# Row fetches tied to the dense expert steps, and gate one-hots built four tokens at a time, in a PEER layer

## The chip, the core and the metric

One core of a Trainium2 chip runs the whole program. The metric is the device time of one execution in microseconds (us).

## The reference, cut to what matters

The model is a two-layer hybrid block followed by a second block; its last layer is a PEER layer (product-key retrieval of experts), and only that layer is touched here. For each of 512 tokens and 8 heads it scores 128 + 128 half keys, takes the best 16 of each half, adds them to 16 x 16 candidates, takes the best 16 of those and forms a softmax gate over them. So each token uses 8 x 16 = 128 of 16384 experts:

```python
cand = (s_top[:, :, 0, :, None] + s_top[:, :, 1, None, :]).reshape(n_tok, PEER_HEADS, -1)
cand_idx = (i_top[:, :, 0, :, None] * PEER_NKEYS + i_top[:, :, 1, None, :]).reshape(...)
best, pos = lax.top_k(cand, PEER_TOPK)
idx = jnp.take_along_axis(cand_idx, pos, axis=-1)
gate = jax.nn.softmax(best, axis=-1)
act = gelu(einsum("td,thkd->thk", tb, u_tab[ib]))      # u_tab, v_tab: 16384 x 1024, float32
out = einsum("thk,thkd->td", gb * act, v_tab[ib])
```

## The kernel before

**Two ways through the same layer.** The first 128 tokens take the sparse way (`gathered`, L1434): for each of their 128 slots an indirect DMA on POOL's queue (L1444) brings one row of 1024 floats for each of the 128 tokens (512 KB), first from table `pur`, later from `pvr`. A `pur` row is multiplied with the token's hidden vector and summed on DVE (L1450); four such dots go through a Gelu on ACT (L1454) and the gate (L1455); then each `pvr` row is added to `acc`, scaled, on DVE (L1459). All rows use four buffers of one tag, `er`. That makes 256 fetches and 256 uses.

The other 384 tokens take the dense way: all 16384 experts are computed with matmuls and masked by a gate matrix. The 128 chunks of 128 experts are in 16 groups of 8. For each group there are 8 *e-steps* (`expert`, L1482: a 512 KB weight tile is loaded by SP at L78, split into a high and a low part on ACT, L84, and DVE, L85, 24 matmuls of 384 columns follow at L106, then a product on DVE, L1486, and a Gelu on ACT, L1488; POOL multiplies with the gate tile, L1515; ACT, L92, and DVE, L93, split the result into `eh` and `el`) and 8 *m-steps* (weight tile as before, 24 matmuls that read `eh` and `el`, and an addition to the residual on DVE, L1535). So a weight tile goes with 24 matmuls in both kinds. The groups run in the order 4 to 15, then 0 to 3. The 32 chunks of groups 0 to 3 are computed early, inside the stage that builds the gate matrix (`ahead`, L1493), and stored; their e-steps later only load the stored activations, so these four groups have matmuls in their m-steps alone. The gate tile `gt` of a group is loaded by SP at L1508, with two buffers, so the load for a group is issued when POOL has done the last product of the group two places earlier.

**The gate stage** (`pairs`, L1574) runs over four tiles of 128 tokens. For each tile: candidates on POOL, the top 16 of each head on DVE, the two half positions from `pos` by a shift and a mask on unsigned integers with a cast each (L1590 to L1593), two one-hot selections over 128 x 2048 (`eq`: compare on DVE, L1595, product on POOL, L1596, sum on DVE, L1597), and the softmax. For tile 0 this ends in `eidx` and `egate`, the indices for the fetches. For tiles 1 to 3 the gate matrix is built token by token: `lt` is the one-hot row of the first half index times the gate (DVE, L1633, one instruction per token), `rt` the one-hot of the second half index (two tokens on ACT by Square and Relu, L1625 and L1629; two on POOL, L1627), their outer product is a matmul of 128 columns (L1634), and four tokens are copied out of PSUM by ACT (L1635). There are 96 such packs of four tokens, 32 per tile; a pack sits in a block of four, and each of the 24 blocks is stored to DRAM.

**What sets the order.** The program is written as one sequence, and the framework's planner orders each engine's instructions by its own estimate of time: of the instructions that it takes to be ready, the one that stands first in the program goes first. `gathered` is a generator; `more(n)` takes n of its steps, a step being one fetch and its use. The calls put 10 steps over the 8 e-steps of a group and 8 over its m-steps, but nothing ties them there: a fetch goes out as soon as a buffer is free, and a use as soon as its row is expected.

Of the kernel before, what the change touches and what calls it, by code (L numbers as in the profile page):

```python
# [9 lines left out]
F = mybir.dt.float32  # L10
# [16 lines left out]
D = 1024  # L27
# [3 lines left out]
SPT = 128  # L31
DW = 512 - SPT
EARLY = 4
EPS = 1e-6
# [9 lines left out]
class K:  # L44
# [1389 lines left out]
    def gathered(self, ht):  # L1434

        nc, mp, a = self.nc, self.mp, self.a
        NB = 4
        acc = mp.tile([128, D], F, name="acc")
        nc.gpsimd.memset(acc, 0.0)
        self.acc = acc  # L1440

        def fetch(table, s):
            r = mp.tile([128, D], F, name="er", tag="er", bufs=4)
            nc.gpsimd.indirect_dma_start(r, None, a[table], bass.IndirectOffsetOnAxis(ap=self.eidx[:, s:s + 1], axis=0))  # L1444
            return r
        for b in range(0, 128, NB):
            dot = mp.tile([128, NB], F, name="dot", bufs=2)
            for i in range(NB):
                r = fetch("pur", b + i)
                nc.vector.tensor_tensor_reduce(out=r, in0=r, in1=ht, scale=1.0, scalar=0.0, op0=OP.mult, op1=OP.add,  # L1450
                                               accum_out=dot[:, i:i + 1])
                if i == NB - 1:
                    w = mp.tile([128, NB], F, name="ew", bufs=2)
                    nc.scalar.activation(w, dot, AF.Gelu)  # L1454
                    nc.vector.tensor_mul(w, w, self.egate[:, b:b + NB])  # L1455
                yield
            for i in range(NB):
                r = fetch("pvr", b + i)
                nc.vector.scalar_tensor_tensor(acc, r, w[:, i:i + 1], acc, op0=OP.mult, op1=OP.add)  # L1459
                yield  # L1460

    def peer(self):
# [6 lines left out]
        with tc.tile_pool(name="peer", bufs=1) as mp:  # L1469
            self.mp = mp  # L1470
            io = mp.tile([128, 144], F, name="io")
            nc.sync.dma_start(io, a["iota"])
            sel = [mp.tile([128, DW], F, name=f"sel{i}") for i in range(4)]
            ht = self.by_token(rc)
# [22 lines left out]
            with tc.tile_pool(name="topk", bufs=1) as tp:  # L1497
                self.topk(tp, hh, hl, rr, io, sel, gd, ahead)
            with tc.tile_pool(name="exp", bufs=1) as ep:
                groups = list(range(EARLY, 16)) + list(range(EARLY))  # L1500
                for g in groups:
                    wh, wl = [], []
                    last = g == groups[-1]
                    for e in range(8):
                        j = g * 8 + e
                        if e == 0:
                            gt = ep.tile([128, DW // TB, 8, TB], F, name="gt", bufs=2)
                            nc.sync.dma_start(gt, gd[:, :, j:j + 8, :])  # L1508
                        if g < EARLY:
                            act = mp.tile([128, DW], F, name="act", bufs=4)  # L1510
                            nc.sync.dma_start(act, ad[j])
                        else:
                            act = expert(j)
                        av = act.rearrange("p (b t) -> p b t", t=TB)
                        nc.gpsimd.tensor_mul(av, av, gt[:, :, e, :])  # L1515
                        h = ep.tile([128, DW], FR, name="eh", bufs=11)
                        q = ep.tile([128, DW], FR, name="el", bufs=11)
                        self.hilo(act, h, q)
                        wh.append(h)
                        wl.append(q)  # L1520
                        more(0 if last else 2 if e % 4 == 0 else 1)
                    if g == groups[-2]:
                        more(256)
                    for m in range(8):
# [17 lines left out]

    def topk(self, sp, hh, hl, rr, io, sel, gd, ahead):

# [24 lines left out]
        with tc.tile_pool(name="topk2", bufs=1) as mp:  # L1569
            self.pairs(mp, sv, sif, io, sel, gd, ahead)  # L1570

    def pairs(self, mp, sv, sif, io, sel, gd, ahead):
        nc = self.nc
        b3, b4 = [128, 8, 16], [128, 8, 16, 16]  # L1574
        for t in range(4):
# [9 lines left out]
            res = [mp.tile(b3, F, name=f"res{i}", bufs=1) for i in range(3)]  # L1585
            pi = mp.tile(b3, U32, name="pi", bufs=1)
# [26 lines left out]
            for i in range(3):  # L1613
                nc.vector.tensor_copy(sel[i][:, s0:s0 + 128], pt[:, i * 128:i * 128 + 128])
            neg = sel[3]
            nc.vector.tensor_scalar(neg[:, s0:s0 + 128], pt[:, 128:256], -1.0, None, op0=OP.mult)
            for tb in range(s0 // TB, (s0 + 128) // TB):
                st = mp.tile([128, 128, TB], F, name="stage", bufs=2)
                for t4 in range(TB // 4):
                    ps = self.bank("g")  # L1620
                    rt = mp.tile([128, 4, 128], F, name="rt", bufs=2)
                    for u in range(4):
                        i = tb * TB + t4 * 4 + u
                        if u < 2:
                            nc.scalar.activation(rt[:, u], io[:, 0:128], AF.Square, bias=neg[:, i:i + 1])  # L1625
                        else:
                            nc.gpsimd.tensor_scalar(rt[:, u], io[:, 0:128], sel[1][:, i:i + 1], None, op0=OP.is_equal)  # L1627

                    nc.scalar.activation(rt[:, 0:2], rt[:, 0:2], AF.Relu, scale=-1.0, bias=1.0)  # L1629
                    for u in range(4):  # L1630
                        i = tb * TB + t4 * 4 + u
# [179 lines left out]
```

## Time and profile before

| | us |
|---|---|
| Median of 3 runs | 4869.48 (4867.33 to 4875.77) |
| The profiled execution: its own time | 4869.11 |
| The profiled execution: its span | 4867.3 |
| PE busy in the span | 4532.7 (93%) |
| DVE busy in the span | 3264.9 (67%) |
| ACT busy in the span | 1948.5 (40%) |
| POOL busy in the span | 1127.8 (23%) |

The profile is that of one execution. The gate stage lies from about 3420 to 3764 us in the span, the dense groups from there to about 4850. PE is TensorE, DVE is VectorE, ACT is ScalarE, POOL is GpSimd, SP is the engine whose queue issues most DMAs. The granted clock is the share of TensorE's full speed that the chip gave in a stretch.

### The profile page before, as it was taken

The numbers are of one execution on the slowest core, as the hardware profiler recorded it, in microseconds if no ns is written. First come the engines' busy times: TensorE is split into PE (matmuls) and PEld (weight loads), VectorE is DVE, ScalarE is ACT, GpSimd is POOL, SyncE is SP. The second block draws the span as 40 slices with busy tenths as digits, with TensorE's granted clock in tenths as the row PEclk, the third lists the DMA queues.
The fourth block names the chain that finished last, engine by engine and source line by source line (L and its number), as shares of the span: only waits on it lengthen the run. The fifth ranks groups of instructions, "written<-read, shape, count | busy, mean of one in ns | idle before, by whom it ended". The sixth has DMA issues, their size and how long they took to land. (4 is left out here: it accounts for less than half of the span.)

```text
span 4867.3 us, 63592 instructions
## 1 busy us (share of the span) xinstructions
PE 4532.7 (93%) x23070; PEld 3875.8 (80%) x23070; DVE 3264.9 (67%) x6217; ACT 1948.5 (40%) x3439; POOL 1127.8 (23%) x1061
## 2 busy tenths in 40 slices
PE   9999999999999999989999998989788898888998
PEld 7887777788888878767888787867677787887998
DVE  4447878754454468787544477877988888787455
ACT  3235565532232247556322333322387223232333
POOL 0001012210000011132100102223467555553222
PEclk9999999999999999999999998999899899999999
DMA  3234323533332343234333333132346888887454
GB/s 129 93 108 133 89 83 95 165 100 96 97 96 95 95 132 101 88 96 141 121 95 97 114 118 104 49 110 83 118 168 215 294 317 296 301 312 245 151 173 144
DMA packets 276313, 688.33 MB, mean 141 GB/s; under 512 B 32192, under 2 KB 92256, under 8 KB 272928
## 3 DMA queue, kind: packets, MB, share of 16 engines
q1 hardware_dynamic: 239136, 550.02, 35.7%
q0 software_dynamic: 36864, 134.23, 8.0%
q8 instruction: 184, 3.01, 0.3%
q14 instruction: 129, 1.06, 0.1%
HBM read 593.04 MB, written 68.04 MB: 136 GB/s over the span
## 5 line engine op out<-in xcount | busy, mean ns | idle before, releaser
L84 ACT CAST wh<-raw 128x1024 fp32r<-128x1024 f32 (+3 forms) x773 | 766.5, 993 | 1742.0 <-PE bk L106 1082.7
L106 PE MATMUL bk<-hh,wh 128*128 128x512 f32 (+1 forms) x3016 | 1138.6, 378 | 47.7 <-DVE t L1486 19.0
L106 PE MATMUL bk<-hh,wl 128*128 128x512 f32 (+1 forms) x3016 | 1136.3, 377 | 37.0 <-DVE wl L85 36.0
L106 PE MATMUL bk<-hl,wh 128*128 128x512 f32 (+1 forms) x3016 | 1135.0, 376 | 0.3 <-DVE hl L231 0.3
L85 DVE TENSOR_TENSOR wl<-raw,wh 128x1024 fp32r<-128x1024 f32 (+3 forms) x693 | 842.0, 1216 | 155.5 <-ACT wh L84 148.5
L106 PEld LDWEIGHTS bk<-hh,wh 128*128 128x128 f32 x3016 | 573.2, 190 | 137.7 <-issue 28.9
L106 PEld LDWEIGHTS bk<-hh,wl 128*128 128x128 f32 x3016 | 572.1, 190 | 130.8 <-DVE wl L85 51.5
L106 PEld LDWEIGHTS bk<-hl,wh 128*128 128x128 f32 x3016 | 573.8, 190 | 78.7 <-issue 2.4
L106 PE MATMUL bk<-eh,wh 128*128 128x384 f32 x1024 | 355.5, 349 | 55.6 <-ACT eh L92 53.1
L196 POOL TENSOR_TENSOR sq<-sq,sqt 128x512 f32<-128x512 f32 x62 | 104.1, 1679 | 1200.9 <-ACT sqt L192 1182.1
L106 PE MATMUL bk<-el,wh 128*128 128x384 f32 x1024 | 356.0, 348 | 9.5 <-DVE el L93 9.2
L106 PE MATMUL bk<-eh,wl 128*128 128x384 f32 x1024 | 353.0, 345 | 2.2 <-DVE wl L85 2.0
L85 POOL TENSOR_TENSOR wl<-raw,wh 128x1024 fp32r<-128x1024 f32 (+2 forms) x80 | 185.4, 2318 | 578.8 <-ACT wh L84 458.7
L106 PE MATMUL bk<-gh,wh 128*128 128x512 f32 x704 | 273.9, 389 | 0.0
L106 PE MATMUL bk<-gh,wl 128*128 128x512 f32 x704 | 273.9, 389 | 0.0
L106 PE MATMUL bk<-gl,wh 128*128 128x512 f32 x704 | 273.9, 389 | 0.0
L106 PEld LDWEIGHTS bk<-eh,wh 128*128 128x128 f32 x1024 | 197.8, 194 | 66.7 <-ACT eh L92 63.0
L255 DVE TENSOR_TENSOR t<-bk,rr 128x512 f32<-128x512 f32 x88 | 60.8, 691 | 269.2 <-PE bk L106 269.2
L1515 POOL TENSOR_TENSOR act<-act,gt 128x384 f32<-128x384 f32 x128 | 168.2, 1320 | 291.1 <-ACT act L1488 174.8
L264 DVE SCALAR_TENSOR_TENSOR x<-bk,x 128x512 f32<-128x512 f32 x96 | 66.4, 692 | 231.6 <-PE bk L106 231.6
L106 PEld LDWEIGHTS bk<-el,wh 128*128 128x128 f32 x1024 | 198.5, 194 | 18.4 <-DVE el L93 18.0
L106 PEld LDWEIGHTS bk<-eh,wl 128*128 128x128 f32 x1024 | 199.0, 194 | 5.3 <-DVE wl L85 5.1
(699 smaller groups left out, 8778.2 us busy)
## 6 DMA issues: line engine op xcount, KB each, us to landing
raw<-in_wi SPq DMA_DIRECT2D x176, 512.0 KB
raw<-in_pu SPq DMA_DIRECT2D x128, 512.0 KB
raw<-in_pv SPq DMA_DIRECT2D x128, 512.0 KB
raw<-in_wo SPq DMA_DIRECT2D x64, 448.0 KB
raw<-in_mg SPq DMA_DIRECT2D x48, 512.0 KB
gate_d<-stage SPq DMA_DIRECT2D x24, 1024.0 KB
gt<-gate_d SPq DMA_DIRECT2D x16, 1536.0 KB
raw<-in_wo SPq DMA_DIRECT2D x32, 512.0 KB
```

The costliest lines, as they stand in the source:

```text
L84: self.nc.scalar.copy(wh[:, :n], raw[:, :n])
L85: (eng or self.nc.vector).tensor_sub(wl[:, :n], raw[:, :n], wh[:, :n].bitcast(F))
L106: self.nc.tensor.matmul(ps, x[:, c], y[k], start=(n == 0), stop=(n == 3 * kk - 1))
L196: nc.gpsimd.tensor_add(self.sq, self.sq, t)
L255: nc.vector.tensor_mul(t2, pb, rr)
L264: nc.vector.scalar_tensor_tensor(self.x[m], ps, 0.5, self.x[m], op0=OP.mult, op1=OP.add)
L1515: nc.gpsimd.tensor_mul(av, av, gt[:, :, e, :])
```

## The change

The generator is rewritten. It now lists all 256 steps first, with the four `pvr` rows of a block of slots behind the four `pur` rows of the next block, and it issues the fetch of step n together with the use of step n - 3. Each fetch and each use is passed through `keep_in_program_order`, which puts it behind the instruction written just before it on its engine; later instructions may still be moved ahead of it. Counting the three last uses there are 259 calls. One is made behind each of the 24 blocks of the gate stage, one behind every e-step but those of the last group, one behind every m-step of groups 4 to 15, and the rest in one go behind the e-steps of the last group but one (`more(256)`).

In the gate stage `lt` becomes one compare for four tokens, without the gate; the gate moves into `rt`: token 0 on ACT (Square, then Relu with the gate as scale and bias), token 1 on DVE, tokens 2 and 3 on POOL, each a compare and a product in one instruction. The half positions come from one cast and float arithmetic (a rounding by adding and subtracting a constant) ahead of both selections.

```diff
     def gathered(self, ht):
-        NB = 4
+        order = self.tc.keep_in_program_order
+        NB, LOOK = 4, 3
...
+        for b in range(nb + 1):
+            steps += [("pur", NB * b + i) for i in range(NB) if b < nb] + [("pvr", NB * (b - 1) + i) for i in range(NB) if b]
+        rows, dots, ws = {}, {}, {}
+        for n in range(len(steps) + LOOK):
+            if n < len(steps):
+                table, s = steps[n]
+                r = rows[n] = mp.tile([128, D], F, name="er", tag="er", bufs=LOOK + 1)
+                order(nc.gpsimd.indirect_dma_start(r, None, a[table], bass.IndirectOffsetOnAxis(ap=self.eidx[:, s:s + 1], axis=0)))
+            if n >= LOOK:
+                table, s = steps[n - LOOK]
+                r, b, i = rows.pop(n - LOOK), s // NB, s % NB
+                if table == "pur":
...
+                    order(nc.vector.tensor_tensor_reduce(out=r, in0=r, in1=ht, scale=1.0, scalar=0.0, op0=OP.mult, op1=OP.add,
+                                                         accum_out=dots[b][:, i:i + 1]))
...
+                else:
+                    order(nc.vector.scalar_tensor_tensor(acc, r, ws[b][:, i:i + 1], acc, op0=OP.mult, op1=OP.add))
+            yield
...
-                        more(0 if last else 2 if e % 4 == 0 else 1)
+                        more(0 if last else 1)
                     if g == groups[-2]:
                         more(256)
...
-                        more(0 if g >= groups[-2] else 1)
+                        more(1 if g >= EARLY else 0)
...
-            for x in range(2):
-                if x == 0:
-                    nc.vector.tensor_scalar(pi, pos, 4, None, op0=OP.logical_shift_right)
-                else:
-                    nc.vector.tensor_scalar(pi, pos, 15, None, op0=OP.bitwise_and)
-                nc.vector.tensor_copy(pf, pi)
+            nc.vector.tensor_copy(pf, pos)
+            nc.vector.tensor_scalar(pa, pf, -7.5, 0.0625, op0=OP.add, op1=OP.mult)
+            nc.vector.tensor_scalar(pa, pa, ROUND, ROUND, op0=OP.add, op1=OP.subtract)
+            nc.vector.scalar_tensor_tensor(pf, pa, -16.0, pf, op0=OP.mult, op1=OP.add)
+            for x, pf in enumerate((pa, pf)):
...
+                    lt = mp.tile([128, 4, 128], F, name="lt", bufs=2)
+                    nc.vector.tensor_tensor(lt, io[:, 0:128].unsqueeze(1).to_broadcast(bc), sel[0][:, i:i + 4].unsqueeze(2).to_broadcast(bc),
+                                            op=OP.is_equal)
                     for u in range(4):
-                        if u < 2:
-                            nc.scalar.activation(rt[:, u], io[:, 0:128], AF.Square, bias=neg[:, i:i + 1])
+                        g = sel[2][:, i + u:i + u + 1]
+                        if u == 0:
+                            nc.scalar.activation(rt[:, u], io[:, 0:128], AF.Square, bias=sel[3][:, i + u:i + u + 1])
+                            nc.scalar.activation(rt[:, u], rt[:, u], AF.Relu, scale=sel[4][:, i + u:i + u + 1], bias=g)
                         else:
-                            nc.gpsimd.tensor_scalar(rt[:, u], io[:, 0:128], sel[1][:, i:i + 1], None, op0=OP.is_equal)
-                    nc.scalar.activation(rt[:, 0:2], rt[:, 0:2], AF.Relu, scale=-1.0, bias=1.0)
+                            (nc.vector if u == 1 else nc.gpsimd).tensor_scalar(rt[:, u], io[:, 0:128], sel[1][:, i + u:i + u + 1], g, op0=OP.is_equal, op1=OP.mult)
                     for u in range(4):
-                        lt = mp.tile([128, 128], F, name="lt", bufs=4)
-                        nc.vector.tensor_scalar(lt, io[:, 0:128], sel[0][:, i:i + 1], sel[2][:, i:i + 1], op0=OP.is_equal, op1=OP.mult)
-                        nc.tensor.matmul(ps[:, u * 128:u * 128 + 128], lt, rt[:, u], start=True, stop=True)
+                        nc.tensor.matmul(ps[:, u * 128:u * 128 + 128], lt[:, u], rt[:, u], start=True, stop=True)
...
                 ahead(1 if t < 3 and tb % 2 == 0 else 0)
+                more(1)
```

## Rows read from the trace of the kernel before

**Rows 1.** Busy time of the engines (instructions), granted clock, DMA share, GB/s by stretch.
```profile
3520.00:3560.00 40.00, 36.06 (x242) 31.93 (x241) 35.43 (x123) 39.36 (x85) 26.52 (x38) 1.00 0.52 192
...
3764.00:3801.00 37.00, 26.25 (x122) 22.64 (x120) 26.76 (x31) 11.31 (x19) 19.76 (x17) 0.82 0.93 300
3801.00:4476.00 675.00, 581.62 (x3070) 547.22 (x3070) 563.35 (x700) 199.00 (x285) 357.87 (x295) 0.95 0.86 299
...
4546.00:4613.00 67.00, 66.84 (x384) 66.44 (x384) 32.99 (x40) 24.06 (x33) 13.05 (x8) 1.00 0.48 150
```
**Rows 2.** SP's gate-tile loads in order of time: start us, duration us, instruction.
```profile
3800.83 0.53 SPq L1508 DMA_DIRECT2D gt<-gate_d  x1
...
4476.20 0.53 SPq L1508 DMA_DIRECT2D gt<-gate_d  x1
4545.58 0.53 SPq L1508 DMA_DIRECT2D gt<-gate_d  x1
4612.85 0.53 SPq L1508 DMA_DIRECT2D gt<-gate_d  x1
4683.15 0.53 SPq L1508 DMA_DIRECT2D gt<-gate_d  x1
```
**Rows 3.** The fetches of L1444 alone: stretch, POOL busy (fetches), clock, DMA.
```profile
3801.00:4476.00 675.00, 277.08 (x231) 0.95 0.86 299
```
**Rows 4.** Waits from 3800 to 4400: total us, times, longest us.
```profile
PE bk L106 <- ACT eh L92: 42.8, 15, 3.8
DVE er L1450 <- DMA er<-in_pur,eidx: 41.6, 17, 6.5
```
**Rows 5.** One group's end in order of time, from PE, DVE and POOL.
```profile
4040.49 0.33 PE L106 MATMUL bk<-hh,wl 128*128 128x384 f32 x1
...
4048.66 0.54 DVE L1486 TENSOR_TENSOR t<-bk,rr 128x384 f32<-128x384 f32 x1
...
4050.01 1.25 POOL L1444 DMA_INDIRECT er<-in_pur,eidx  x1 [2.83 <-ACT act L1488]
...
4052.97 1.01 PE L106 MATMUL bk<-eh,wh 128*128 128x384 f32 x2 [3.18 <-ACT eh L92]
```
**Rows 6.** Groups of instructions, 3800 to 4400: busy us, mean ns, idle before.
```profile
L1459 DVE SCALAR_TENSOR_TENSOR acc<-er,ew,acc 128x1024 f32<-128x1024 f32 x107 | 150.5, 1407 | 24.3 <-DMA er<-in_pvr,eidx 23.3
L85 DVE TENSOR_TENSOR wl<-raw,wh 128x1024 fp32r<-128x1024 f32 x114 | 149.7, 1313 | 11.7 <-ACT wh L84 11.3 <-issue 0.4
L1450 DVE CUSTOM_DVE_ANT_0 er<-er,ht 128x1024 f32<-128x1024 f32 x106 | 140.3, 1331 | 41.8 <-DMA er<-in_pur,eidx 41.6
```
**Rows 7.** A fetch on POOL, and the DVE instruction that waited for its row.
```profile
4002.08 0.94 POOL L1444 DMA_INDIRECT er<-in_pur,eidx  x1 [0.85 <-DVE acc L1459]
...
4008.35 1.22 DVE L1450 CUSTOM_DVE_ANT_0 er<-er,ht 128x1024 f32<-128x1024 f32 x1 [0.82 <-DMA er<-in_pur,eidx]
```
**Rows 8.** Gate-stage groups of instructions, 3520 to 3560, by engine.
```profile
L1635 ACT COPY stage<-g 128x512 f32<-128x512 f32 x19 | 19.9, 1050 | 0.5 <-PE g L1634 0.5
L1625 ACT ACTIVATE rt<-io,sel 128x128 f32<-128x128 f32 x38 | 13.0, 396 | 0.0
L1629 ACT ACTIVATE rt<-rt 128x256 f32<-128x256 f32 x20 | 8.4, 422 | 0.2
...
L1633 DVE TENSOR_SCALAR lt<-io,sel,sel 128x128 f32<-128x128 f32 x75 | 21.1, 344 | 4.6 <-PE g L1634 4.4
...
L1627 POOL TENSOR_SCALAR rt<-io,sel 128x128 f32<-128x128 f32 x38 | 26.6, 711 | 12.4 <-PE g L1634 9.2 <-ACT rt L1629 3.0
```
**Rows 9.** The page's groups: a DVE instruction over 512 columns.
```profile
L255 DVE TENSOR_TENSOR t<-bk,rr 128x512 f32<-128x512 f32 x88 | 60.8, 691 | 269.2 <-PE bk L106 269.2
```
**Rows 10.** Tile 1's selections in order of time: DVE's cast and POOL's product.
```profile
3489.70 2.29 DVE L1595 TENSOR_TENSOR eq<-pf,io 128x2048 f32<-128x2048 f32 x1
...
3492.24 5.32 DVE L1593 CAST pf<-pi 128x128 f32<-128x128 uint32 x1
...
3492.83 4.63 POOL L1596 TENSOR_TENSOR eq<-eq,sif 128x2048 f32<-128x2048 f32 x1
```

More of the change, by code (lines that the diff above doesn't have):

```diff
@@ L32 @@
 DW = 512 - SPT
+ROUND = 1.5 * 2.0 ** 23
 EARLY = 4
@@ L1436, in gathered @@
         nc, mp, a = self.nc, self.mp, self.a
-        NB = 4
-        acc = mp.tile([128, D], F, name="acc")
+        order = self.tc.keep_in_program_order
+        NB, LOOK = 4, 3
+        acc = self.acc = mp.tile([128, D], F, name="acc")
         nc.gpsimd.memset(acc, 0.0)
[L1440 to L1460, printed above, removed]
+        nb = 128 // NB
@@ new lines, in gathered @@
+        steps = []
+        for b in range(nb + 1):
[10 more added lines that the diff above has]
+                if table == "pur":
+                    if i == 0:
+                        dots[b] = mp.tile([128, NB], F, name="dot", bufs=2)
+                    order(nc.vector.tensor_tensor_reduce(out=r, in0=r, in1=ht, scale=1.0, scalar=0.0, op0=OP.mult, op1=OP.add,
+                                                         accum_out=dots[b][:, i:i + 1]))
+                    if i == NB - 1:
+                        w = ws[b] = mp.tile([128, NB], F, name="ew", bufs=3)
+                        nc.scalar.activation(w, dots.pop(b), AF.Gelu)
+                        nc.vector.tensor_mul(w, w, self.egate[:, NB * b:NB * b + NB])
+                else:
+                    order(nc.vector.scalar_tensor_tensor(acc, r, ws[b][:, i:i + 1], acc, op0=OP.mult, op1=OP.add))
+            yield
@@ L1472, in peer @@
             nc.sync.dma_start(io, a["iota"])
-            sel = [mp.tile([128, DW], F, name=f"sel{i}") for i in range(4)]
+            sel = [mp.tile([128, DW], F, name=f"sel{i}") for i in range(5)]
             ht = self.by_token(rc)
@@ L1497, in peer @@
             with tc.tile_pool(name="topk", bufs=1) as tp:
-                self.topk(tp, hh, hl, rr, io, sel, gd, ahead)
+                self.topk(tp, hh, hl, rr, io, sel, gd, ahead, more)
             with tc.tile_pool(name="exp", bufs=1) as ep:
@@ L1541, in peer, with topk @@
                             self.x[m] = t
-    def topk(self, sp, hh, hl, rr, io, sel, gd, ahead):
+    def topk(self, sp, hh, hl, rr, io, sel, gd, ahead, more):
         nc, tc, a = self.nc, self.tc, self.a
@@ L1569, in topk, with pairs @@
         with tc.tile_pool(name="topk2", bufs=1) as mp:
-            self.pairs(mp, sv, sif, io, sel, gd, ahead)
-    def pairs(self, mp, sv, sif, io, sel, gd, ahead):
+            self.pairs(mp, sv, sif, io, sel, gd, ahead, more)
+    def pairs(self, mp, sv, sif, io, sel, gd, ahead, more):
         nc = self.nc
@@ L1585, in pairs @@
             res = [mp.tile(b3, F, name=f"res{i}", bufs=1) for i in range(3)]
-            pi = mp.tile(b3, U32, name="pi", bufs=1)
             pf = mp.tile(b3, F, name="pf", bufs=1)
-            for x in range(2):
-                if x == 0:
-                    nc.vector.tensor_scalar(pi, pos, 4, None, op0=OP.logical_shift_right)
-                else:
-                    nc.vector.tensor_scalar(pi, pos, 15, None, op0=OP.bitwise_and)
-                nc.vector.tensor_copy(pf, pi)
+            pa = mp.tile(b3, F, name="pa", bufs=1)
+            nc.vector.tensor_copy(pf, pos)
[3 more added lines that the diff above has]
+            for x, pf in enumerate((pa, pf)):
                 e = mp.tile(b4, F, name="eq", tag="big", bufs=2)
@@ L1614, in pairs @@
                 nc.vector.tensor_copy(sel[i][:, s0:s0 + 128], pt[:, i * 128:i * 128 + 128])
-            neg = sel[3]
-            nc.vector.tensor_scalar(neg[:, s0:s0 + 128], pt[:, 128:256], -1.0, None, op0=OP.mult)
+            nc.vector.tensor_scalar(sel[3][:, s0:s0 + 128], pt[:, 128:256], -1.0, None, op0=OP.mult)
+            nc.vector.tensor_scalar(sel[4][:, s0:s0 + 128], pt[:, 256:384], -1.0, None, op0=OP.mult)
             for tb in range(s0 // TB, (s0 + 128) // TB):
```

4 lines of the change are left out of this document (2 added, 2 removed).

## The prediction

> **What bounds the kernel now.** I read the busy time by stretch first, then the order of one engine's own DMA issues, then the waits, and last the order of time around one stall. In the table by stretch [rows 1] the reader is to compare two lines. From 4546 to 4613 no rows are fetched any more: PE is busy 66.84 of 67.00 us, its granted clock is 1.00 and the DMA share 0.48. From 3801 to 4476 rows are fetched: PE is busy 582 of 675 us, the clock is 0.95, DMA is at 0.86 and DVE at 563 of 675. So PE's matmuls bound the end of the kernel, and the middle loses time on top of them.
>
> How much shows in the gate-tile loads, one for each group of 16 weight tiles [rows 2]. From 3800.83 to 4476.20 there are eight periods, 84.4 us each; the one from 4545.58 to 4612.85 is 67.27 us, that is 4.20 us for a weight tile with its 24 matmuls. The eleven full groups from 3800.83 to 4683.15 take 882.3 us; eleven of 67.27 would be 740.0, so 142 us are in play. In the slow eight, 231 fetches were issued [rows 3], 28.9 a group, so one costs (84.4 - 67.27) / 28.9 = 0.59 us of PE's time.
>
> The waits say why [rows 4]: PE waits for `eh`, up to 3.8 us at once, and DVE itself stands 41.6 us in front of rows that have not landed. Around one group's end the chain can be seen [rows 5]. The last matmul of an expert starts at 4040.49, but the product `t` of the last expert runs on DVE at 4048.66, behind row uses; POOL then has a fetch of 1.25 us in its queue ahead of the gate product, and PE resumes at 4052.97. After such a stop the clock is below 1.00, which is the 5% of the stretch.
>
> **Part 1, the fetches tied to the steps.** A full group gets 16 fetches and 16 uses in place of 28.9. What they cost: a use 1.33 or 1.41 us of DVE (1.37 in the mean), beside `wl` with 1.31 [rows 6] and about 0.55 for each 384-column DVE instruction [rows 5], and a fetch 0.94 us of POOL [rows 7]. DVE in an e-step: 1.31 + 2 x 0.55 + 1.37 + 0.08 (an accumulator read, estimated) = 3.86 of 4.20 us; in an m-step 1.31 + 0.55 + 1.37 = 3.23. That is 84% at PE's full pace, no lower a share than today, but without the standing: fetch n goes out three steps ahead of its use, 3 x 4.20 = 12.6 us, and a row fetched at 4002.08 could be used at 4008.35, 6.3 us later, with DMA at 0.86 [rows 1, 7]. DMA gets easier too: 32 transfers of 0.52 MB and a gate tile of 1.57 MB are 18.4 MB a group, 256 GB/s against 299 now. POOL's fetch waits for the buffer that the use of the step before frees; behind it stands the next gate product, behind the use stand `t` and `wl`. So at a group's end the last expert's chain (`t`, Gelu, gate product, `eh`, `el`) can still meet one use on DVE (1.37) and one fetch on POOL (0.94), 2.3 us together.
>
> Per group the bounds are 0 (rows hidden) and 16 x 0.59 = 9.5 us (the price of today kept). I take 4.5 us: the 2.3 us once, a wait for `wl` of about the same size as one use on the way (1.4), and 0.8 for the clock after it. That is 71.8 us a group, 11 x 71.8 = 790: **92 us less**. What is late next is again `eh` at the group's end, only shorter.
>
> The first dense stretch (3764 to 3801, PE 26.25 of 37 us, clock 0.82, DMA 0.93 [rows 1]) holds the first gate tiles together with a burst of fetches. One fetch a step takes the burst away; I count **4 us less**, bounds 0 and 10.
>
> **Part 2, what moves to the end.** Of 259 steps 24 go to the gate stage, 12 x 16 = 192 to groups 4 to 15, 24 to the e-steps of groups 0 to 2, and 19 are left for one go behind the e-steps of group 2: 43 steps where today there is none. The 24 lie beside e-steps without matmuls, while PE does the m-steps of the group before (33.6 us for 8 tiles). DVE there needs 8 x (1.31 + 0.55 + 0.55 + 1.37) = 30 us, but the uses stand between the `el` that PE wants one after the other; I take 0.33 us a step, 8 us. The 19 have to be done before the last group adds `acc`, one group of 33.6 us later. DVE then needs 19 x 1.45 + 8 x (1.31 + 0.55) + 8 x 0.55 = 47 us, 13 too many, and 16 fetches at the spacing of today (675 / 231 = 2.9 us) take 47 us as well. Neighbours take up a part; 9 us. Together **17 us more**, bounds 5 and 0.59 x 43 + 13 = 39.
>
> **Part 3, the gate stage.** In its steady part ACT is busy 39.36 of 40 us and makes 19 packs, 2.1 us each, 96 packs in 202 us; PE is busy 36.06 [rows 1, 8]. ACT's three instructions for `rt`, 2 x 0.396 + 0.422, become two of 128 columns, about 0.79, so a pack costs it 0.42 less and ACT is no longer last. DVE: 4 x 0.344 = 1.38 becomes one instruction over 512 columns, for which the nearest row is 0.69 [rows 9], and one of 0.344: 0.34 less, which the 24 uses (24 x 1.37 / 96 = 0.34) take back. POOL keeps two instructions, now compare and product. No row shows that form: between 0.71 as today and twice that. I take 0.8, as it is the same pass over 128 columns; with a fetch per four packs (0.24) POOL is at 1.84 of 2.1 us and hides. PE is then the bound, at most 3.94 / 19 = 0.2 us a pack or 20 us over all; DVE (35.43 of 40) is close behind, so I take 5 us.
>
> Between tiles the second cast stands 5.32 us on DVE beside POOL's product of 4.63 [rows 10]; it is now made before both selections. If the compare that follows (2.29 us) started at once, POOL's second product could come 3 us earlier, in four tiles 12 us. The Trainium skill, SBUF — State Buffer, section Who interferes with whom, speaks against that: the port pair that VectorE shares with GpSimd is held whole by one of them, and a VectorE instruction with two SBUF inputs stands as well while GpSimd reads. The compare has two, so by the rule it only inherits the cast's place; the sum by the rule is 4782, without it 4773. For the sum itself I take the removed instructions alone, 0.7 us a tile, 3 us. Part 3: **8 us less**, bounds 23 less and, with POOL's instruction at twice 0.711, 2 x 1.42 + 0.24 = 3.1 against 2.1 us a pack, up to 94 more.
>
> **Sum.** 4869.1 (the profiled execution; its span is 4867.3, and the median of the runs 4869.5, so no correction) - 92 - 4 + 17 - 8 = 4782.
>
> **The rivals.**
>
> *A, the price per row stays.* If a row costs PE 0.59 us wherever it runs, eleven groups take 11 x (67.27 + 9.5) = 845, 38 less; the 43 late steps cost 25 more; with part 3, 4869 - 38 + 25 - 8 = 4848. For it: DVE's share stays at 84%. Against: part of the price is standing before unlanded rows, and three steps cover 6.3 us.
>
> *B, rows cost nothing at one a weight tile.* -142 - 10 + 5 - 23: 4699. For it: 4546 to 4613 has slack on all engines but PE. Against: the chain at a group's end has none.
>
> *C, POOL becomes the bound of the gate stage.* It decides from (2.1 - 0.24) / 2 = 0.93 us an instruction; at 1.3 a pack takes 2.84 us, 71 us more in place of 5 less: 4858, hence still within or just above no change. Against: POOL idles 12.4 of 40 us [rows 8].
>
> *D, slower: the pins lengthen every expert's chain.* Place: the e-steps, where the use is queued behind `el` and the fetch behind the gate product. If PE cannot cover them, every e-step costs up to 1.37 + 0.94 = 2.3 us: a group takes 67.27 + 18.5 = 85.8, eleven 61 more than now, the 24 early e-steps 55 and the last go 13 more, and with the 12 less of the first stretch and part 3 it is 4986. It decides at x us exposed an e-step where -142 + 88 x + 24 x + 13 - 12 = 0, x = 1.26. For it: PE's stops are already in this chain [rows 5]. Against: three PSUM banks and three weight tiles let PE run two tiles, 8.4 us, ahead.
>
> **How the numbers follow.** Forecast 0.53, alone 4750 to 4815; A 0.18, B 0.07, C 0.10, D 0.12. The range 4735 to 4860 takes in A and most of C, and leaves out D and most of B, not quite 2 in 10. No change means within 0.2%, 10 us, about what a measurement of this kernel can tell. Faster: the forecast, B, most of A and half of C, 0.81; same: the rest of A and C but the worst, 0.06; slower: D and the worst of C, 0.13.
>
> **What would show it.** Right: gate-tile loads of groups 5 to 15 evenly 70 to 74 us apart; a clock near 0.98 and PE over 95% there; DVE's wait for rows almost gone; ACT below 90% in the gate stage; a stop of PE near the end where `acc` is transposed. Wrong: periods near 77 (A) or 85 (D); POOL's `rt` at 0.93 us and more, with POOL busy throughout the gate stage (C); no uses of rows after 4476 would mean that the pins don't hold.

## The result: slower by 1%, and the profile after

The changed kernel takes 4919.59 us (median of 4 runs, 4917.05 to 4921.86) against 4868.4 us before (4 runs beside them): ratio 1.0102, 95% interval 1.0085 to 1.012. The prediction was 4782. Its profiled execution has a span of 4920.0 us, against 4867.3 before.

Four marks cut the two spans into the parts that the prediction names: the start of the last stage copy of the gate stage (the last number of the times in the two lines that follow, before and after), the two gate-tile loads between which the eleven full groups lie (3800.83 and 4683.15 in [rows 2]; 3857.53 and 4690.37 below), and the end of the span.

```profile
L1635 ACT COPY stage<-g x96: 1017/1048/1102, 3514.5 to 3761.2; 128x512 f32<-128x512 f32 x96
```
```profile
L1644 ACT COPY stage<-g x96: 1015/1051/1089, 3520.6 to 3817.5; 128x512 f32<-128x512 f32 x96
```

| part | before, us | after, us | difference | predicted |
|---|---|---|---|---|
| gate stage, up to its last copy | 3761.2 | 3817.5 | +56 | -8 |
| from there to the first full group | 39.6 | 40.0 | 0 | -4 |
| eleven full groups | 882.3 | 832.8 | -49 | -92 |
| the rest | 184.2 | 229.6 | +45 | +17 |

Busy time by stretch after, with the columns of [rows 1]: a piece of the gate stage, the first dense stretch, ten full groups, and the end in three pieces.

```profile
3520.00:3560.00 40.00, 31.32 (x197) 26.99 (x197) 26.66 (x54) 30.94 (x54) 39.38 (x36) 1.00 0.56 189
3824.00:3858.00 34.00, 26.46 (x133) 25.06 (x131) 24.86 (x27) 11.57 (x19) 17.28 (x16) 0.85 0.87 268
3858.00:4610.00 752.00, 701.47 (x3836) 688.86 (x3836) 501.40 (x662) 246.38 (x341) 307.45 (x241) 0.96 0.75 246
4690.00:4737.00 47.00, 37.73 (x192) 35.38 (x190) 36.42 (x44) 10.86 (x17) 26.22 (x21) 0.86 0.83 276
4737.00:4775.00 38.00, 35.65 (x193) 35.17 (x193) 33.12 (x39) 12.11 (x18) 18.37 (x16) 0.92 0.89 310
4775.00:4920.00 145.00, 112.83 (x576) 104.90 (x576) 99.24 (x139) 39.42 (x57) 65.16 (x48) 0.87 0.63 212
```

In the gate stage POOL (the fifth busy time) is now at 39.38 of 40 us; before it was ACT with 39.36 [rows 1]. In the full groups PE is busy 93%, better than the 86% of [rows 1], but DVE has much slack, 501 of 752, and PE still isn't full. SP's gate-tile loads after, which answer to [rows 2]:

```profile
3857.53 0.53 SPq L1515 DMA_DIRECT2D gt<-gate_d  x1
...
4234.47 0.53 SPq L1515 DMA_DIRECT2D gt<-gate_d  x1
4309.49 0.53 SPq L1515 DMA_DIRECT2D gt<-gate_d  x1
...
4609.79 0.53 SPq L1515 DMA_DIRECT2D gt<-gate_d  x1
4690.37 0.53 SPq L1515 DMA_DIRECT2D gt<-gate_d  x1
```

Nine of the eleven periods are 74.2 to 75.1 us, where before eight of 84.4 stood beside short ones; the first is 78.3 and the last 80.6. So the pins hold the pace, and the pace of 75.0 is 7.7 us above PE's 67.27.

**The gate stage.** Groups of instructions from 3520 to 3560 after, as in [rows 8]:

```profile
L1641 POOL TENSOR_SCALAR rt<-io,sel,sel 128x128 f32<-128x128 f32 x33 | 37.5, 1143 | 0.1
L1643 PE MATMUL g<-rt,lt 128*128 128x128 f32 x133 | 21.6, 293 | 8.7 <-POOL rt L1641 7.7 <-ACT rt L1639 0.9
...
L1644 ACT COPY stage<-g 128x512 f32<-128x512 f32 x16 | 16.9, 1058 | 8.4 <-PE g L1643 8.4
L1632 DVE TENSOR_TENSOR lt<-io,sel 128x512 f32<-128x512 f32 x16 | 11.8, 737 | 11.2 <-PE g L1643 11.1
L1639 ACT ACTIVATE rt<-rt,sel,sel 128x128 f32<-128x128 f32 x16 | 7.9, 491 | 0.3
```

POOL's compare-and-multiply takes 1143 ns here (1.11 us over all 192), not 711 [rows 8] and not the 0.8 of the forecast, and PE waits for it. 16 packs fit where 19 did.

**A group's end.** From the timeline of all engines, one e-step of a full group and what PE does at the end of the group's e-steps (start, duration, instruction, idle time before it):

```profile
4225.45 0.56 DVE L94 TENSOR_TENSOR el<-act,eh 128x384 fp32r<-128x384 f32 x1 [1.45 <-ACT eh L93]
...
4225.93 1.28 DVE L1466 SCALAR_TENSOR_TENSOR acc<-er,ew,acc 128x1024 f32<-128x1024 f32 x1
...
4227.12 0.55 DVE L1493 TENSOR_TENSOR t<-bk,rr 128x384 f32<-128x384 f32 x1
...
4227.70 0.53 ACT L1495 ACTIVATE act<-t 128x384 f32<-128x384 f32 x1 [1.33 <-DVE t L1493]
...
4228.38 1.29 POOL L1522 TENSOR_TENSOR act<-act,gt 128x384 f32<-128x384 f32 x1 [2.37 <-ACT act L1495]
...
4229.69 0.51 ACT L93 CAST eh<-act 128x384 fp32r<-128x384 f32 x1 [1.46 <-POOL act L1522]
...
4230.24 0.56 DVE L94 TENSOR_TENSOR el<-act,eh 128x384 fp32r<-128x384 f32 x1 [1.44 <-ACT eh L93]
...
4230.26 0.44 PE L107 MATMUL bk<-eh,wh 128*128 128x384 f32 x1 [0.89 <-ACT eh L93]
...
4235.04 0.69 PE L107 MATMUL bk<-eh,wh 128*128 128x384 f32 x1 [3.57 <-ACT eh L93]
```

This is a closed loop. The row use is pinned behind `el`, the next `t` stands behind the use on DVE, and Gelu, product, `eh` and the next `el` follow one after the other: 4230.24 - 4225.45 = 4.79 us from `el` to `el`, of which DVE itself idles 1.44. PE needs 4.18 us for a tile. PE runs ahead, as the forecast said, but the chain falls 0.6 us further behind in each of eight e-steps, and PE stands for the sum at the end (0.89 and 3.57 us, when the first m-step asks for the last two `eh`). After the longer stop the granted clock is 0.50, half of full speed (1.2 in place of 2.4 GHz): 18 matmuls start in 6 us. In e4, the run below that takes the stop away, the same 6 us hold 37. The two rows, after the change and in e4, with the columns of [rows 1]:

```profile
4235.00:4241.00 6.00, 5.96 (x18) 5.66 (x19) 4.50 (x7) 1.04 (x1) 2.39 (x3) 0.50 0.83 250
```
```profile
4235.00:4241.00 6.00, 6.00 (x37) 6.00 (x36) 5.95 (x8) 2.61 (x5) 4.59 (x4) 1.00 0.83 312
```

**The end.** From the timeline, in the e-steps of group 0:

```profile
4724.46 1.23 DVE L1459 CUSTOM_DVE_ANT_0 er<-er,ht 128x1024 f32<-128x1024 f32 x1 [2.09 <-DMA er<-in_pur,eidx]
...
4725.61 0.55 DVE L94 TENSOR_TENSOR el<-act,eh 128x384 fp32r<-128x384 f32 x1
...
4726.22 0.69 PE L107 MATMUL bk<-el,wh 128*128 128x384 f32 x1 [4.76 <-DVE el L94]
```

PE waits 4.76 us for an `el` that is queued on DVE behind a use whose row has not landed. Over the whole end, PE's busy time grows from 168.8 to 185.8 us for the same matmuls, as the granted clock is 0.88 in place of 0.96, and its standing from 15.4 to 43.8. So of the 45 us some 17 are the clock's and 28 are waits, of which those for `wl` (9.3) and `el` (8.3) are the longest.

### The profile page after: what moved, and what is told of

The parts are those of the page before. It is cut to its first block, busy times and chain, and to the rows that moved or that the text cites. A ratio compares the mean times of both kernels' runs of the same rounds, so it can differ in the third digit from the quotient of the medians.

```text
span 4920.0 us, 63316 instructions
## 1 busy us (share of the span) xinstructions
PE 4557.3 (93%) x23070; PEld 3912.1 (80%) x23070; DVE 3198.9 (65%) x6028; ACT 1935.8 (39%) x3343; POOL 1213.8 (25%) x1061
## 3 DMA queue, kind: packets, MB, share of 16 engines
q14 instruction: 128, 1.05, 0.1%
## 5 line engine op out<-in xcount | busy, mean ns | idle before, releaser
L86 DVE TENSOR_TENSOR wl<-raw,wh 128x1024 fp32r<-128x1024 f32 (+3 forms) x693 | 830.1, 1199 | 159.1 <-ACT wh L85 150.4
L107 PE MATMUL bk<-eh,wh 128*128 128x384 f32 x1024 | 366.5, 359 | 71.6 <-ACT eh L93 51.9
L107 PE MATMUL bk<-el,wh 128*128 128x384 f32 x1024 | 365.9, 358 | 12.2 <-DVE el L94 11.0
```

Of the source, the lines that this page charges most:

```text
L86: (eng or self.nc.vector).tensor_sub(wl[:, :n], raw[:, :n], wh[:, :n].bitcast(F))
L107: self.nc.tensor.matmul(ps, x[:, c], y[k], start=(n == 0), stop=(n == 3 * kk - 1))
```

## The experiments

The theory: three losses of their own, the POOL instruction in the gate stage, the loop through DVE in the full groups, and the 43 late steps at the end. The first two were undone alone; the end was mended on top of the mended groups; then all came together. The cuts of code are shortened.

**1. Which part of the change holds the gate stage.** Only the one-hot tiles and the selection arithmetic undone; then only these put into the kernel before.

```diff
e1, on the kernel after (e2 is the reverse, on the kernel before)
-  nc.vector.tensor_tensor(lt, io (broadcast), sel[0] (broadcast), is_equal)             # one for four tokens
+  nc.vector.tensor_scalar(lt, io, sel[0], sel[2], is_equal, mult)                       # one for each token
-  rt: u = 0 on ScalarE, u = 1 on VectorE, u = 2, 3 on GpSimd with is_equal and mult
+  rt: u = 0, 1 on ScalarE, u = 2, 3 on GpSimd with is_equal alone
```

> The changed kernel with the one-hot tiles and the selection arithmetic of the kernel before; the fetches stay as changed, the 24 steps in the gate stage among them. Theory: the gate stage lost its 56 us because POOL's compare-and-multiply takes 1.10 us, not 0.8. With the one-operation compare back (0.71) POOL has slack, ACT sets the pace again and the last stage copy comes at 3758 to 3772 in place of 3817.5; groups stay at 75.0 us and the end at 229 us: 4860 to 4880 us. Rival: the 24 fetches and uses put into the gate stage are what slows it; then it stays above 3800 and the time above 4900.

Measured: 4894.33 us, ratio to before 1.0051 (1.0031 to 1.0072); last stage copy at 3786.4; groups 75.0.

> The kernel before with the new one-hot tiles and selection arithmetic alone; fetches as before. Theory: POOL's two instructions of 1.10 us set the pace of the gate stage, 2.2 us a pack without the fetch that the changed kernel adds (0.98 for four packs): 70 to 72 us for 32 packs in place of 64 (75 to 80 with the fetch), so the stage is 18 to 30 us longer and the kernel 4885 to 4900 us. Rival: the one-hot form costs the whole 56 us by itself (a stop elsewhere in it, such as the wait for the wider tile): 4920 to 4930.

Measured: 4884.99 us, 1.0032 (1.0018 to 1.0047); last stage copy at 3780.8; the three tiles, each from the first to the last of its 32 stage copies, 64.2, 65.8 and 80.7 us (63.6, 63.6 and 64.6 before).

The first missed its range, for the stage and for the time. The second lies at the lower edge of its range, but not in the way of its theory: two tiles are almost as short as before and one is much longer. Busy time of its first and third tile, columns as in [rows 1]:

```profile
3513.00:3578.00 65.00, 53.74 (x342) 48.27 (x342) 49.52 (x127) 56.87 (x99) 63.78 (x61) 0.94 0.44 168
...
3700.00:3781.00 81.00, 62.11 (x356) 54.23 (x355) 52.08 (x88) 58.11 (x102) 79.19 (x70) 0.93 0.58 199
```

In both POOL is busy nearly all the time; in the first no fetch runs, in the third nine fetches and ten uses. So the new form fills POOL without yet lengthening the tile, and what fetches and uses add then shows in full.

Neither edit alone makes the 56 us: the new one-hot form alone costs 20 (3780.8 - 3761.2; the profiled execution is 9 us above the median of its runs, so 20 is rather high), the steps alone 25 (3786.4 - 3761.2), both together at least 11 more than the sum. So the 24 steps, which the prediction cost at nothing, are a loss as large as that of the new form. Without it they lengthen the first tile (71.4 us) and the gaps between tiles (33 and 36 us, 28 and 27 before); what in a step costs this was not separated.

**2. What makes POOL's instruction long.** Three edits of the changed kernel:

```diff
e3: tokens 2 and 3 compared alone on POOL, their gate value on lt
-  gpsimd.tensor_scalar(rt[:, u], io, sel[1], g, is_equal, mult)
+  gpsimd.tensor_scalar(rt[:, u], io, sel[1], None, is_equal)
+  vector.tensor_scalar(lt[:, u], io, sel[0], sel[2], is_equal, mult)    # u = 2, 3; a 256-column compare for 0, 1
e8: lt by four compares with one tensor input
-  vector.tensor_tensor(lt, io (broadcast), sel[0] (broadcast), is_equal)
+  vector.tensor_scalar(lt[:, u], io, sel[0], None, is_equal)            # u = 0 .. 3
e12: POOL's compare alone, and nothing in its place
-  gpsimd.tensor_scalar(rt[:, u], io, sel[1], g, is_equal, mult)
+  gpsimd.tensor_scalar(rt[:, u], io, sel[1], None, is_equal)
```

> The changed kernel with POOL's two one-hot tiles made by the compare alone; the gate value of these two tokens is multiplied in on VectorE, on the other factor. Theory: POOL's instruction falls from 1.10 to about 0.65 us, POOL takes 2 x 0.65 + 0.25 = 1.55 us a pack, VectorE about 0.45 + 3 x 0.34 + 0.34 = 1.8, ACT 0.79 + 1.05 = 1.84, PE about 1.9: a tile of 32 packs takes 60 to 65 us in place of 75 to 80, the gate stage ends 45 to 65 us earlier: 4855 to 4875 us. Rival (the 512-column compare or the port that VectorE and POOL share holds the stage): a tile stays above 70 us and the time above 4895.

Measured: 4896.18 us, 1.0048 (1.0029 to 1.0067). A tile took 58 to 60 us, a little less than expected, but the gaps between tiles grew to 41 and 50 us (30 and 37 after). DVE has more to do for the packs here; that it comes later to the next tile's selection for that reason is likely, but was not shown. The stage ended at 3784.3, 33 us earlier, but 14 of these were lost again before the first full group, which began 54 us after the last copy, not 40. The time missed its range by 21 us.

> The changed kernel with lt made by four compares of 128 columns with one tensor input, in place of one of 512 columns with two; POOL's compare-and-multiply stays. Theory: that instruction takes 0.78 us where nothing stands beside it and is stretched while VectorE runs an instruction with two tensor inputs, lt among them; with one-input compares beside it its mean falls from 1.10 to 0.82 to 0.90 us, POOL to about 2.0 us a pack, a tile to 64 to 68 us, and the time by 20 to 40: 4880 to 4900. Rival: the second operation costs 1.10 us by itself, whatever VectorE does: mean 1.05 to 1.15, a tile 74 to 80, 4915 to 4930.

Measured: 4919.81 us, 1.0101 (1.0079 to 1.0123): no gain. The time and the mean (1.03) missed the theory; the time is the rival's, but its reason does not hold, as the lines below show.

> The changed kernel with POOL's two instructions of a pack made as the compare alone; the gate value of these two tokens is left out, and no other engine gets work for it. Theory: the second operation on POOL makes POOL the last engine of a pack (1.10 us against 0.75 for the compare alone). Without it POOL needs 2 x 0.75 + 0.3 = 1.8 us a pack, a tile of 32 packs takes 60 to 64 us in place of 75 to 80, and since VectorE gets no work the gaps between tiles stay at 30 to 37: the last stage copy at 3775 to 3787, 4880 to 4892 us. Rival: the wide compare or ScalarE's second instruction holds the pack, a tile stays at 70 or more: above 4903.

Measured: 4893.79 us, 1.0046 (1.003 to 1.0063), last stage copy at 3793.4, a tile 67 to 69 us: all somewhat beyond the theory's ranges, and on its side of the rival's. So POOL's second operation alone makes 24 us (3817.5 - 3793.4) of the 31 that taking back the whole form gives (3817.5 - 3786.4, e1).

The 192 instructions of POOL's line in each, before, after, e8 and e12 in this order (count, then shortest, median and longest in ns, first and last start):

```profile
L1627 POOL TENSOR_SCALAR rt<-io,sel x192: 590/630/2636, 3509.5 to 3759.1; 128x128 f32<-128x128 f32 x192
```
```profile
L1641 POOL TENSOR_SCALAR rt<-io,sel,sel x192: 780/1050/2990, 3517.6 to 3816.1; 128x128 f32<-128x128 f32 x192
```
```profile
L1641 POOL TENSOR_SCALAR rt<-io,sel,sel x192: 781/872/3908, 3514.5 to 3817.2; 128x128 f32<-128x128 f32 x192
```
```profile
L1641 POOL TENSOR_SCALAR rt<-io,sel x192: 590/691/2529, 3518.8 to 3792.2; 128x128 f32<-128x128 f32 x192
```

The shortest show the price alone: 0.59 us for one operation, 0.78 for two; after the change the 25 with nothing on DVE beside them took 0.78 to 0.80. So the forecast's 0.8 was right for an instruction that runs alone; the rest of the median of 1.05 is stretching. With one-input compares beside it (e8) the median falls to 0.87: the wide two-input `lt` stretches POOL. It is the smaller part, though. After the change the 192 instructions took 64 us more than 0.78 each; 43 of that lie with the 57 that ran beside a row use or a `wl`, and 21 with the 100 that ran beside `lt` and neither of these. All that took over 1.56 us are of the first kind. Through them the mean over all 192 stays at 1.03 us in e8 (0.74 before, 1.11 after, 0.94 in e12); the gaps between tiles there grow as well (35 and 45 us), so nothing is won.

**3. The loop.** The step of an e-step moved ahead of the gate product, so that the use stands behind `t` and not behind `el`:

```diff
                             act = expert(j)
+                        more(0 if last else 1)
                         av = act.rearrange("p (b t) -> p b t", t=TB)
...
                         wl.append(q)
-                        more(0 if last else 1)
```

> The changed kernel with the fetch-and-use step of an e-step moved ahead of the gate product, so that the use is queued on VectorE behind t and not behind el. Theory: t, Gelu, gate product, eh, el and the use form a loop of 4.78 us from expert to expert, longer than PE's 4.18, and PE pays 8 x 0.6 us and the clock after it at each group's end. With the use beside Gelu and the product the loop is 3.6 us, PE is the bound, and the eleven groups take 67.5 to 69.5 us each in place of 75.0: 60 to 82 us less, 4838 to 4860 us. Rival: the loss is the fetch in POOL's queue or VectorE's total load; then the fetch, which now stands ahead of this expert's product, keeps the period at 73 to 78 and the time is 4900 to 4950.

Measured: 4842.32 us, 0.994 (0.9923 to 0.9956). Busy time of ten of its full groups, columns as in [rows 1]:

```profile
3922.00:4595.00 673.00, 669.23 (x3845) 666.03 (x3844) 559.92 (x662) 246.53 (x341) 361.64 (x241) 1.00 0.79 274
```

Periods of 66.5 to 67.4 us, below what the theory gave: PE's floor [rows 1, 2], with the clock at 1.00 and 16 rows a group fetched and used. One e-step of it:

```profile
4232.78 0.55 DVE L94 TENSOR_TENSOR el<-act,eh 128x384 fp32r<-128x384 f32 x1
...
4233.37 0.56 DVE L1493 TENSOR_TENSOR t<-bk,rr 128x384 f32<-128x384 f32 x1
4233.85 1.22 DVE L1459 CUSTOM_DVE_ANT_0 er<-er,ht 128x1024 f32<-128x1024 f32 x1
...
4234.82 1.11 POOL L1523 TENSOR_TENSOR act<-act,gt 128x384 f32<-128x384 f32 x1 [1.10 <-ACT act L1495]
...
4234.98 2.03 DVE L86 TENSOR_TENSOR wl<-raw,wh 128x1024 fp32r<-128x1024 f32 x1
...
4236.94 0.55 DVE L94 TENSOR_TENSOR el<-act,eh 128x384 fp32r<-128x384 f32 x1
```

The use now lies beside Gelu and the gate product. From `el` to `el` it is 4.16 us, PE's own pace. The eleven groups take 739.2 us, 94 less than after the change. The end grew to 244.5 us (229.6), for a reason that was not looked for, so the kernel gains 77. The fetch now stands ahead of the product, and the period fell all the same: the rival is out, and the place of the use behind `el` was the loss.

**4. The end.** On the kernel of e4, second steps in some m-steps: two a group, so that 19 steps are left for the e-steps of groups 0 to 2 and none for one go (e7), or four a group, so that none is left (e5).

```diff
-                        more(1 if g >= EARLY else 0)
+                        more(0 if g < EARLY else 2 if m in (1, 3, 5, 7) else 1)     # e5; (3, 7) in e7
and in e5 alone
-                        more(0 if last else 1)                                      # in the e-steps
+                        more(1 if g >= EARLY else 0)
-                    if g == groups[-2]:
+                    if g == 15:
                         more(256)
```

> The kernel of e4_use_before_product with no row step left for the end: a second step in every other m-step of groups 4 to 15, none after group 15. Theory: the end (from the last full group's load on) is 45 to 60 us longer than before because of its 43 late steps; without them it is 184 us again in place of 244.5, while the groups still hide their 20 steps (an m-step has 4.18 us of PE against 3.1 of VectorE and 1.3 for the second use): periods 67 to 70, 4775 to 4815 us. Rival: twenty steps a group are too many for the transfers or for VectorE, and each extra one costs the 0.59 us of the kernel before: periods 69.5 and more and 4805 to 4830; or the end is long for another reason and stays at 230 or more: above 4840.

Measured: 4788.1 us, 0.9838 (0.9814 to 0.9861); the end 191.3 us, 7 above the 184 of the theory.

> The kernel of e4_use_before_product with 18 row steps in a full group in place of 16, so that 19 steps are left for the e-steps of groups 0 to 2 and none in one go behind them. Theory: the lump of 19 is the larger part of the long end, since the last group's m-steps wait for it: the end falls from 244.5 to 200 to 220 us and the time to 4800 to 4820. Rival: the steps in the e-steps of groups 0 to 2 are the cost, each 1.3 us on VectorE between el and el: the end stays at 230 to 240, 4830 to 4840.

Measured: 4807.08 us, 0.9869 (0.9848 to 0.9891); the end 209.3 us.

So, with the steps placed as in e4, the lump and the five steps ahead of it cost 35 us (244.5 - 209.3) and the 19 steps among the e-steps 18 (209.3 - 191.3), 0.95 each. PE's waits from 4597 to 4780 in e4 and in e5 (total us, times, longest us):

```profile
PE bk L107 <- DVE el L94: 19.1, 6, 10.1
PE bk L107 <- DVE ew L1464: 8.1, 2, 5.3
```
```profile
PE bk L107 <- DVE el L94: 1.2, 3, 0.4
```

The standing before `el` goes with the late steps. In the groups the extra rows cost nothing; ten groups of e5:

```profile
3922.00:4595.00 673.00, 668.84 (x3842) 665.65 (x3841) 606.40 (x726) 248.10 (x346) 399.85 (x280) 1.00 0.87 305
```

Twenty rows a group, DMA at 0.87 and 305 GB/s, and still 67.3 us a group: the transfers were not what made the groups long, and rival A's 0.59 us for every row is refuted.

**5. What the pins do.**

```diff
-        order = self.tc.keep_in_program_order
+        order = lambda x: x
```

> The changed kernel without the pins: fetches and uses are written at the same places, and the planner orders them as it did before. Theory: it pulls them forward again, 25 to 29 a group; the loop from expert to expert is broken but the row waits return: periods of 80 to 87 us for seven or eight groups, then 67; the end is 184 to 190 us; with the slow gate stage 4895 to 4925 us. Rival: the fetch and use order changes nothing that the pins hold; periods of 75 us throughout and 4915 to 4925.

Measured: 4914.59 us, 1.0095 (1.007 to 1.0121). Seven periods of 77 to 87 us and four of 67 to 70, and an end of 184 us. The planner pulls the rows forward as before, and DVE waits for them (50.8 us from 3878 to 4455). With the steps at these places the pins move the loss from the groups to the end and are worth nothing in sum. Whether PE would also run full at the places of e4 and e5 without them was not run.

**6. Put together.** The kernel of e5 with the old one-hot form (e10); with the steps of the gate stage moved into the groups, 22 in each (e11); and between the two, 8 steps in the gate stage and 21 a group (e13).

```diff
e11, on e10
-                        more(0 if g < EARLY else 2 if m in (1, 3, 5, 7) else 1)
+                        more(0 if g < EARLY else 2 if m in (1, 2, 3, 4, 5, 6) else 1)
-                more(1)                            # in the gate stage
e13, on e10: m in (1, 2, 4, 5, 7), and in the gate stage
+                more(1 if tb % 3 == 0 else 0)
```

> The kernel of e5_none_late with the one-hot tiles and the selection arithmetic of the kernel before, and the 24 row steps still in the gate stage. Theory: the 31 us that the gate stage loses to the new one-hot form on top of the steps (3817.5 against 3786.4 in e1_old_onehot) come off, and the groups stay at 67.3: 4754 to 4766 us. Rival: the form costs only the 20 us that it cost without the steps (e2_only_onehot): 4766 to 4772.

Measured: 4759.96 us, 0.9772 (0.9751 to 0.9793); last stage copy at 3789.7.

> The kernel of e10_both_mended with the 24 row steps of the gate stage moved into the full groups, 22 in each in place of 20. Theory: the steps cost the gate stage 25 us (3786.4 against 3761.2 before), and in the groups the rows are still hidden behind PE (20 of them took nothing: 67.3 us a group): the stage ends near 3761, 4728 to 4742 us. Rival: with two uses in six of eight m-steps VectorE needs 8 x (1.62 + 0.55) + 14 x 1.3 = 35.6 us against 33.6 of PE, or the DMA engines, at 0.87 already, can't carry two more rows: periods of 69 to 71 us, and 4750 to 4780.

Measured: 4759.94 us, 0.9768 (0.974 to 0.9796). The stage ends at 3761.6, 28 us earlier: that is the price of 24 steps there. So the theory's time is missed: the groups take 68.2 to 71.8 us and give the gain back, as its rival had it:

```profile
4000.00:4500.00 500.00, 485.40 (x2748) 480.14 (x2747) 450.07 (x545) 179.74 (x252) 311.83 (x216) 0.99 0.87 309
```

PE has lost its full share, while DVE is at 450 of 500 and DMA at the same 0.87 as in e5. The longest waits of DVE from 3900 to 4500 are for PE (21.5 us) and for rows (25.7 in sum, 13.3 in e10); whether DVE's load or late rows come first was not separated.

> The kernel of e10_both_mended with 8 row steps in the gate stage in place of 24, and 21 in a full group in place of 20. Theory: a step in the gate stage costs about 1 us (25 for 24), and the groups pay for the rows only where 22 are too many (2.0 us a group in e11_no_gate_steps): the stage ends near 3770, periods 67.3 to 68.3: 4738 to 4752 us. Rival: the price in a group rises in proportion, 1 us for the 21st: 4750 to 4760, no better than either.

Measured: 4755.05 us, 0.9766 (0.975 to 0.9783): 3 us beyond the theory and inside the rival's range. The stage ends at 3765.4, as the theory had it, but the periods go up to 70.1 us. The three can't be told apart. All are 2.3% faster than the kernel before and some 3% faster than the changed one.

## Why the prediction was wrong

**The reading of what bounds the kernel was right.** PE's floor of 67.27 us a group was reached with rows in the stream (e4, e5), and the 142 us in play in eleven groups were there: e4 takes 143 less than before.

**Part 1 failed at the sentence "So at a group's end the last expert's chain ... can still meet one use on DVE (1.37) and one fetch on POOL (0.94), 2.3 us together".** The use was charged once a group. It stands in the loop of every e-step, at 4.79 us against PE's 4.18, and eight lags of 0.6 us arrive together: 4.46 us of standing. The clock was taken at 0.8 us; PE is busy for 701.5 us in ten groups where the same matmuls take 669.2 in e4, 3.2 us a group. Together 7.7, which is the 7.7 measured, in place of 4.5; the longer first and last period make 9 us more. The mechanism is rival D's and at its place, with 0.6 us where D had up to 2.3 and needed 1.26 to make the kernel slower. So D as priced was wrong, and its objection (PE runs two tiles ahead) was right for each e-step and wrong for their sum. The fetch is not in the loop: POOL idles 2.37 us before the product. The sum of DVE's busy time, 3.86 of 4.20, could not show this; only the order of its queue could.

**Part 2 had the places and not the sizes.** What failed are its terms "0.33 us a step, 8 us" for the 24 steps and 9 for the lump; the measured +45 lies even beyond its upper bound of 39. Their split is known only with the steps placed as in e4: 0.95 us a step among the e-steps, and up to 35 us for the lump. The prediction let neighbours take up a part of the standing. In the lines above a row is late instead (2.09 us), `el` waits behind its use, and PE's clock falls to 0.88 after such stops, for which Part 2 had no term. PE's stop where `acc` is transposed was only 1.0 us.

**Part 3 failed at "I take 0.8, as it is the same pass over 128 columns" and at the 24 uses "take back" 0.34 us a pack with nothing lost.** The first is the price of the instruction alone. In the stage it is 1.11 in the mean: beside the two-input `lt` that the same edit puts on DVE, and more so beside the row uses and `wl`. Rival C's rule then gives 2 x 1.11 + 0.24 = 2.46 us a pack; measured 75 to 79 us from the first to the last copy of a tile, 2.42 to 2.55 a pack, against 2.05 to 2.08 before. That makes 37 of the 56 us; the gaps (30 and 37 us against 28 and 27) and a start 6 us later make the rest. The prediction had C's condition (0.93) and gave it a tenth. The second is refuted by e1: the steps alone cost 25 us.

**The first dense stretch** took as long as before, 40.0 against 39.6 us, where 4 less were forecast. Seven fetches fall in it in place of nine, so there was hardly a burst to take away; what bounds it was not asked.

**What held.** ACT is at 77% in the gate stage, DVE's wait for rows in the groups is gone, and the first selection product is as forecast: POOL's product starts beside the second compare and takes 6.55 us in place of 4.63 [rows 10]:

```profile
3604.22 2.29 DVE L1602 TENSOR_TENSOR eq<-pf,io 128x2048 f32<-128x2048 f32 x1
```
```profile
3604.39 6.55 POOL L1603 TENSOR_TENSOR eq<-eq,sif 128x2048 f32<-128x2048 f32 x1 [8.21 <-DVE eq L1602]
```

From the first product's start to the second's it is 6.5 us in place of 7.1: the removed instructions alone, as taken. So the compare inherited the cast's place and no 3 us were won: the product is 2.0 us longer than the shortest of its kind (4.53) and runs 2.1 us beside the compare. The Trainium skill, SBUF — State Buffer, section Who interferes with whom, says that a VectorE instruction with two SBUF inputs contends with a GpSimd instruction that reads SBUF; the 6.55 us agree, and so does the median of e8. That one of the two holds the port pair whole, as the prediction put it, fits this compare; beside `lt` it does not, as the 100 instructions that ran beside it grew by 21 us in 37 us of overlap. The prediction weighed this rule for the compare and did not ask it of `lt`, where the change turned four one-input instructions into one with two inputs.

**The sum.** The errors by part are +64 (gate stage), +4 (first stretch), +43 (groups) and +28 (end): 139 us, from 4782 to 4921. Of the mechanisms D named the loop and C named POOL; the price of the steps in the gate stage was taken at nothing. All four errors go in one direction and turned the sign. What would have raised the forecast without any run is the loop, as each of its instructions ran in the kernel before. There `t` (0.55), Gelu (0.53), the product (1.26), `eh` (0.51), `el` (0.55) and a use (1.37) make 4.77 us against PE's 4.20, and the trace of before shows the loop itself, here with 5.2 us from `el` to `el`:

```profile
4119.70 0.55 DVE L93 TENSOR_TENSOR el<-act,eh 128x384 fp32r<-128x384 f32 x1
...
4124.92 0.55 DVE L93 TENSOR_TENSOR el<-act,eh 128x384 fp32r<-128x384 f32 x1
...
4130.09 0.55 DVE L93 TENSOR_TENSOR el<-act,eh 128x384 fp32r<-128x384 f32 x1
```

## What to carry to other kernels

Before an instruction is pinned into a repeated step, add up the closed chain from one turn to the next on each in-order queue that it enters, and compare that with the bound engine's period: engines with slack in busy time can still be too slow in a loop, and the lag shows once, at the next hand-over. Pin the filler behind the instruction that starts the long detour (here `t`), not behind the one that ends it. A filler for a paced loop should not be left over for the part where nothing paces it. And when one edit makes an instruction longer on one engine and widens another beside it, price them together.

## What the runs showed of the hardware that was not expected

A compare-and-multiply over 128x128 on POOL takes 0.78 us alone and a compare 0.59, so the second operation costs 0.19 us. Both grow beside VectorE instructions with two tensor inputs, up to 2.99 us for one of 0.78 that ran beside a row use, a `wl` and an `lt`. The stretching goes both ways: in ten groups of e4, the 79 `wl` that ran beside both POOL's gate product and a fetch took 2.02 to 2.05 us, and the 69 beside a fetch alone 1.22. And the granted clock is 1.00 in the mean when the stops of 4.5 us at each group's end are gone; PE's own work then takes 3.2 us a group less.
